# Attention on one core: two score tiles in three PSUM banks, and a third PSUM tile for the transposes

## The chip, the cores and the metric

The kernel runs on one core of a Trainium2 chip. The core has a matrix engine, TensorE (PE in the profile, with PEld for its weight loads), a vector engine (DVE), an activation engine (ACT), GpSimd (POOL) and a sync engine (SP) that here only issues DMAs. Each takes its instructions in the order in which they were laid down; they meet only at semaphores. TensorE writes its results to PSUM, eight banks of 512 float32 values for each of 128 partitions, and VectorE and ScalarE read them there. The metric is the device time of one execution in microseconds (us), the median of several runs.

## The reference

The reference is a two-layer backbone: in each layer a SwiGLU half step, a token mixer (a short convolution in layer 0, grouped-query attention in layer 1) and another SwiGLU half step, every one with a normalisation, a shift and scale before it and a gated residual behind it. 512 latent tokens attend to 768 keys, namely the 512 latent tokens and 256 context tokens. There are 8 query heads and 2 key-value heads of 128 values each. What bears on the change is the attention of one block of 128 queries:

```python
def gqa_block(q, k, v):
    s = jnp.einsum('bqkgd,bskd->bkgqs', q, k).astype(jnp.float32) * (HEAD_DIM ** -0.5)
    p = jax.nn.softmax(s, axis=-1).astype(v.dtype)
    return jnp.einsum('bkgqs,bskd->bqkgd', p, v)
...
    qb = q_l.reshape(b, n_blocks, Q_BLOCK, N_KV_HEADS, GQA_GROUP, HEAD_DIM).transpose(1, 0, 2, 3, 4, 5)
    o_l = lax.map(lambda q_blk: gqa_block(q_blk, k_all, v_all), qb)
    y_lat = o_l @ w_o
```

All of it is in float32; the order in which the keys are taken makes no difference to a softmax or to the weighted sum behind it.

## The kernel before, in words

To keep float32 accuracy every operand of a product is split into a high and a low part (`split`, L205: ScalarE copies the rounded high part, L206, VectorE subtracts it from the source, L207), and every product is three matmuls: high by high, low by high, high by low. Nearly all of the time is the feed-forward products; the attention of layer 1 lies at about 1894 to 2012 us of 2394.

The queries, keys and values are projected first (`qf`, `kh`, `kl`, `vh`, `vl`). Then comes the part that the change touches, `with tc.tile_pool(name="core" ...)` (L1521). It works on 32 blocks, 8 heads by 4 blocks of 128 queries. `blk` is the block in its head, and n counts the blocks from 0 to 31. Three functions make one block:

- `scores(h, blk)` (L1527): six matmuls write the scores of 128 queries by 768 keys to a tile `sc` with the tag C, three of 512 keys (`off` 0, the latent ones) and three of 256 (the context ones), at L1540 to L1542. Then VectorE takes the row maximum (`reduce_max`, L1544, 768 wide) and scales it (L1545), ScalarE takes the exponential with the row sum (L1547, reading the scores again), VectorE the reciprocal of the sum (L1548), and the probabilities `pr`, which lie in SBUF, are scaled by it, on VectorE for even blocks (L1552) and on ScalarE for odd ones (L1550). After the exponential the score tile is free.
- `turn(h, blk, pr)` (L1555): six transposes on TensorE (L1564) bring `pr` to keys by queries, three each into a PSUM tile with the tag T or U (here called a turn's half). Each tile is emptied by a `split` into `ph` and `pl` (L206, L207).
- `values(h, half, ph, pl)` (L1569): 18 matmuls (`mm3`, L883 to L885) multiply the transposed probabilities of two blocks by the values into a tile with the tag O, which is split into `oh` and `ol`.

TensorE's order is written out by hand in the loop at L1588: in iteration n come the scores of block n + 2, the turn of block n, and then, in every even iteration from 2 on, the values of blocks n - 2 and n - 1. From n = 17 on the odd iterations have a `filler` instead, a step of the output projection (12 matmuls of 512, tile `ps_A`). The first two blocks' scores come ahead of the loop, and behind them the last of the value projections (`v_chunk(5, ...)`, 24 matmuls, L1491 to L1493). TensorE and the DMA queue of SP are issued in program order (`ORDERED`, L47); on VectorE and ScalarE a scheduler lays the instructions down in the order in which it takes them to become ready.

The PSUM tiles come from pools, `psum(C=2, T=2, O=1)` and `psum(U=1)` (L1521, L1522). A tag's number is its number of tiles. A score tile is 1024 values wide, of which 768 are used, so it takes two banks: C has 4 banks, T has 2, O and U have 1 each, and together that is all eight. While h < 4 the halves of the turns go T, T, U in rotation (`turns[0] % 3`, L1562), so a tile is used again after three halves. After the fourth head U is closed and its bank goes to the filler. The tile framework sets the semaphore waits: whoever writes a tile waits for those who still read what was in it.

## Time and profile before

| what | value |
|---|---|
| median of 3 runs | 2396.28 us (2395.4 to 2396.76) |
| the profiled execution's own time | 2396.33 us |
| its span, from the first to the last instruction | 2394.0 us |
| TensorE busy over the span | 2372.9 us (99%) |
| VectorE, ScalarE busy over the span | 2031.4 us (85%), 1168.2 us (49%) |
| first matmul of the 1st, 3rd and 20th block's scores | 1894.04, 1899.40, 1950.61 us |
| TensorE's granted clock over the span | 0.999 |

The profile shows one execution. Its rows name a line of the kernel, an engine, an operation, and the tiles as out<-in with the buffer numbers left out; "ps_C" is a tile of the tag C. Matmuls are pipelined: a row's duration is longer than the step to the next row, and the step is what a matmul costs when they follow each other. In a timeline the square brackets give how long the engine was idle before the row, and whom it waited for. The exponential has two rows, the ACTIVATE and an ACTIVATION_READ_ACCUMULATOR that ends it by delivering the row sum.

### The profile page before, as it was taken

How to read it: one execution, taken by the hardware profiler on the slowest of the kernel's cores; microseconds unless marked ns; L12 is line 12 of the kernel's file. 1: busy time of each engine (PE TensorE's matmuls, PEld its weight loads, DVE VectorE, ACT ScalarE, POOL GpSimd, SP SyncE). 2: the span in 40 equal slices, each digit the busy share in tenths (PEclk: the TensorE clock that was granted, in tenths of full speed). 3: DMA queues.
4: the chain of work that ended last, by engine and by line, in shares of the span. 5: the costliest groups of instructions: out<-in, count | busy, mean ns of one | idle time of the engine just before them, and what ended most of it. 6: DMA issues, size and time to landing. Idle time of an engine off the chain costs nothing.

```text
span 2394.0 us, 37639 instructions
## 1 busy us (share of the span) xinstructions
PE 2372.9 (99%) x14303; PEld 2247.7 (94%) x14303; DVE 2031.4 (85%) x4018; ACT 1168.2 (49%) x2198; POOL 135.4 (6%) x256
## 2 busy tenths in 40 slices
PE   9999999999999999999999999999999999999998
PEld 6999999999999999999999999999998889899998
DVE  6989989978988888888887988888778987988887
ACT  5634334355535653433435543343355776555555
POOL 0001101100000001000000001101100000000000
PEclk9999999999999999999999999999999999999999
DMA  9234444430334123423432144444441101133331
GB/s 338 86 112 138 130 128 129 131 115 27 106 106 133 37 66 115 127 93 119 128 103 70 49 128 124 150 137 121 140 132 45 53 10 58 67 110 102 106 107 62
DMA packets 93062, 253.71 MB, mean 106 GB/s; under 512 B 10320, under 2 KB 18640, under 8 KB 92880
## 3 DMA queue, kind: packets, MB, share of 16 engines
q1 hardware_dynamic: 71984, 183.65, 23.8%
q0 software_dynamic: 20352, 67.12, 9.5%
q8 instruction: 112, 1.84, 0.3%
q14 instruction: 70, 0.57, 0.1%
q10 hardware_dynamic: 544, 0.52, 0.1%
HBM read 249.16 MB, written 2.10 MB: 105 GB/s over the span
## 4 chain that ended last, share of the span: by engine, by line
PE 90%; DVE 4%; ACT 3%; DMA 1%; issue 1%; SPq 0%; DVEq 0%; ACTq 0%
PE ps_A L883 16%; PE ps_A L884 16%; PE ps_A L885 16%; PE ps_C L883 11%; PE ps_C L884 11%; PE ps_C L885 11%; PE ps_B L885 3%; PE ps_B L883 3%; PE ps_B L884 3%; PE ps_T L1564 1%; DMA ada<-in_ada_w 0%; DVE f L785 0%; DVE w L207 0%; DMA raw<-in_ffn_w_in 0%; ACT pr L1547 0%
## 5 line engine op out<-in xcount | busy, mean ns | idle before, releaser
L206 ACT ACTIVATE w<-raw 128x512 fp32r<-128x512 f32 (+1 forms) x862 | 523.6, 621 | 708.9 <-PE ps_A L885 219.1
L207 DVE TENSOR_TENSOR w<-raw,w 128x512 fp32r<-128x512 f32 (+1 forms) x862 | 574.6, 680 | 118.0 <-ACT w L206 104.8
L526 POOL DMA_DIRECT2D aw<-in_ada_t x240 | 129.4, 539 | 1367.0 <-DVE mods L547 1078.5
L390 DVE TENSOR_TENSOR raw<-raw,raw 128x512 f32<-128x512 f32 x264 | 181.7, 690 | 9.0 <-DMA raw<-in_ffn_w_in 4.9
L884 PE MATMUL ps_C<-gl,w 128*128 128x512 f32 (+1 forms) x548 | 188.3, 344 | 0.0
L883 PE MATMUL ps_C<-gh,w 128*128 128x512 f32 (+1 forms) x548 | 188.1, 343 | 0.0
L885 PE MATMUL ps_C<-gh,w 128*128 128x512 f32 (+1 forms) x548 | 188.0, 343 | 0.0
L883 PE MATMUL ps_A<-gh,w 128*128 128x512 f32 (+1 forms) x540 | 185.5, 343 | 0.6 <-DVE x L951 0.6
L884 PE MATMUL ps_A<-gl,w 128*128 128x512 f32 (+1 forms) x540 | 185.6, 344 | 0.0
L885 PE MATMUL ps_A<-gh,w 128*128 128x512 f32 (+1 forms) x540 | 185.4, 343 | 0.0
L547 DVE CUSTOM_DVE_ANT_0 ps_S<-aw,silu_row,packed 128x512 f32<-128x512 f32 x208 | 157.1, 756 | 2.3 <-DMA aw<-in_ada_t 0.9
L547 DVE CUSTOM_DVE_ANT_0 ps_S<-aw,silu_row,mods 128x512 f32<-128x512 f32 x208 | 157.1, 755 | 1.0
L951 DVE SCALAR_TENSOR_TENSOR x<-ps_C,gat,x 128x512 f32<-128x512 f32 (+1 forms) x158 | 99.8, 633 | 43.8 <-PE ps_C L885 43.3
L883 PE MATMUL ps_A<-tB11h,w 128*128 128x384 f32 (+1 forms) x400 | 129.6, 324 | 0.2 <-ACT tB11h L807 0.2
L884 PE MATMUL ps_A<-tB11l,w 128*128 128x384 f32 (+1 forms) x400 | 129.1, 323 | 0.2 <-DVE tB11l L808 0.2
L885 PE MATMUL ps_A<-tB11h,w 128*128 128x384 f32 (+1 forms) x400 | 128.8, 322 | 0.0
L883 PE MATMUL ps_C<-tB22h,w 128*128 128x384 f32 (+2 forms) x376 | 121.3, 322 | 0.0
L885 PE MATMUL ps_C<-tB22h,w 128*128 128x384 f32 (+2 forms) x376 | 121.2, 322 | 0.0
L884 PE MATMUL ps_C<-tB22l,w 128*128 128x384 f32 (+2 forms) x376 | 121.2, 322 | 0.0
L951 DVE SCALAR_TENSOR_TENSOR x<-ps_A,gat,x 128x512 f32<-128x512 f32 (+1 forms) x162 | 102.1, 639 | 16.5 <-PE ps_A L885 16.3
L883 PEld LDWEIGHTS ps_A<-gh,w 128*128 128x128 f32 x540 | 102.3, 189 | 14.0 <-issue 1.0
L885 PEld LDWEIGHTS ps_C<-gh,w 128*128 128x128 f32 x548 | 103.8, 189 | 12.3
(486 smaller groups left out, 6931.9 us busy)
## 6 DMA issues: line engine op xcount, KB each, us to landing
raw<-in_ffn_w_in SPq DMA_DIRECT2D x170, 512.0 KB, 3.8
aw<-in_ada_t POOLq DMA_DIRECT2D x240, 256.0 KB, 3.0
raw<-in_ffn_w_out SPq DMA_DIRECT2D x80, 512.0 KB, 4.1
raw<-in_conv_w_in SPq DMA_DIRECT2D x24, 512.0 KB, 3.7
ada<-in_ada_w SPq DMA_DIRECT2D x28, 256.0 KB, 5.3
raw<-in_attn_w_qkv SPq DMA_DIRECT2D x12, 512.0 KB, 4.5
raw<-in_ada_w SPq DMA_DIRECT2D x8, 512.0 KB, 6.3
silu_row<-in_crow POOLq DMA_DIRECT2D x8, 512.0 KB, 4.1
```

The costliest lines, as they stand in the source:

```text
L206: hi = act.activation(dsth, src, AF.Copy)
L207: lo = dve.tensor_tensor(out=dstl, in0=src, in1=dsth.bitcast(F32), op=ALU.subtract)
L390: dve.tensor_tensor(out=quad(o), in0=quad(x), in1=quad(y), op=ALU.subtract)
L526: nc.gpsimd.dma_start(w, a["ada_t"][t, kh, j])
L547: ins = dve.tensor_tensor_reduce(out=junk, in0=w, in1=silu_row[kh][:, v, :], scale=1.0, scalar=total if kh else ada_b[:, i, hm // 2, col : ...
L883: pe.matmul(ps, wh, xh, start=first, stop=False, **kw)
L884: pe.matmul(ps, wh, xl, start=False, stop=False, **kw)
L885: pe.matmul(ps, wl, xh, start=False, stop=last, **kw)
L951: dve.scalar_tensor_tensor(out=x, in0=p[:, o - off : o - off + w], scalar=gat[:, m, v : v + 1], in1=x, op0=ALU.mult, op1=ALU.add)
L1564: pe.transpose(pt[:, c, :], pr[:, (c0 + c) * P : (c0 + c + 1) * P], ident)
```

## The change

The pools become `psum(C=1, T=3, O=1)`. There is now one tile with the tag C, 1536 values wide, which is exactly three banks, and it is made once for all 32 blocks (`both_sets`). Even blocks use its first 768 columns and odd blocks its last 768. So that no matmul's output crosses a bank, an odd block puts its 256 context keys first (columns 768 to 1023, the second half of the middle bank) and its 512 latent keys behind them (columns 1024 to 1535, the third bank); an even block puts 512 latent keys in the first bank and 256 context keys in the first half of the middle bank. `turn` picks each key block from where it now lies. The bank that becomes free is a third tile of the tag T, and the rotation while h < 4 is over four halves, T, T, T, U. The number of instructions that compute, and their sizes, stay as they were.

```diff
-        with tc.tile_pool(name="core", bufs=2) as cp, psum(C=2, T=2, O=1), ExitStack() as more:
+        with tc.tile_pool(name="core", bufs=2) as cp, psum(C=1, T=3, O=1), ExitStack() as more:
             more.enter_context(psum(U=1))
             turns = [0]
+            both_sets = ptile("C", (P, 2 * NT))
+            SETS = (((0, NL), (NL, NX)), ((NX, NL), (0, NX)))
...
-                sc = ptile("C", (P, 1024))[:, :NT]
-                for off, n in ((0, NL), (NL, NX)):
-                    p = sc[:, off : off + n]
+                side = blk % 2
+                sc = both_sets[:, side * NT : side * NT + NT]
+                for (at, n), off in zip(SETS[side], (0, NL)):
+                    p = sc[:, at : at + n]
...
-                    pt = ptile("U" if h < 4 and turns[0] % 3 == 0 else "T", (P, 4, P))[:, :3, :]
+                    pt = ptile("U" if h < 4 and turns[0] % 4 == 0 else "T", (P, 4, P))[:, :3, :]
                     for c in range(3):
-                        pe.transpose(pt[:, c, :], pr[:, (c0 + c) * P : (c0 + c + 1) * P], ident)
+                        key = (c0 + c) * P
+                        (lat_at, _), (ctx_at, _) = SETS[qq]
+                        key += lat_at if key < NL else ctx_at - NL
+                        pe.transpose(pt[:, c, :], pr[:, key : key + P], ident)
```

The built program shows what becomes of the waits. A name in brackets is the engine whose semaphore an instruction waits for, by the number of instructions that it has finished. In the changed kernel the lines of `scores` and `turn` have moved: L1540 to L1542 are now L1543 to L1545, the reduction L1544 is L1547, the scaling of the maximum L1545 is L1548, the exponential L1547 is L1550, the reciprocal L1548 is L1551, the scaling of even blocks L1552 is L1555, and the transposes L1564 are L1570.

First TensorE, at the end of the first block's scores and the begin of the second block's, before:

```order
L1540 MATMUL ps_C<-kh_17962,qh 128x256
L1541 MATMUL ps_C<-kl_17964,qh 128x256
L1542 MATMUL ps_C<-kh_17962,ql 128x256
L1540 MATMUL ps_C<-kh_17962,qh 128x512
L1541 MATMUL ps_C<-kl_17964,qh 128x512
```

and the same place with the change:

```order
L1543 MATMUL ps_C<-kh_17962,qh 128x256
L1544 MATMUL ps_C<-kl_17964,qh 128x256
L1545 MATMUL ps_C<-kh_17962,ql 128x256
L1543 MATMUL ps_C<-kh_17962,qh 128x512 [waits Activation_49]
L1544 MATMUL ps_C<-kl_17964,qh 128x512
```

The order of the matmuls is the same, but the first matmul of the second block's scores now waits for ScalarE, and the value that it waits for is that of the first block's exponential. It is so for all blocks: before, the scores of block m wait for the exponential of block m - 2, which read the same one of the two tiles; now they wait for that of block m - 1. The wait stands at the first of the six matmuls, ahead of the 512 keys and of the 256.

Then VectorE at the same place, from the first block's row maximum on, before:

```order
L1544 TENSOR_REDUCE sm<-ps_C 128x1 [waits DVE_49,PE_49]
L1544 TENSOR_REDUCE sm<-ps_C 128x1 [waits PE_49]
L1545 TENSOR_TENSOR sm<-sm,nrq 128x1 [waits DVE_49] x2
L1548 RECIPROCAL sm<-sm 128x1 [waits Activation_49]
L1552 TENSOR_SCALAR pr<-pr,sm 128x768 [waits DVE_49]
```

and with the change:

```order
L1547 TENSOR_REDUCE sm<-ps_C 128x1 [waits DVE_49,PE_49]
L1548 TENSOR_TENSOR sm<-sm,nrq 128x1 [waits DVE_49]
L1551 RECIPROCAL sm<-sm 128x1 [waits Activation_49]
L1555 TENSOR_SCALAR pr<-pr,sm 128x768 [waits DVE_49]
L1547 TENSOR_REDUCE sm<-ps_C 128x1 [waits PE_49]
```

The second block's row maximum has moved from ahead of the first block's reciprocal to behind the scaling of its probabilities.

Last TensorE's transposes of one odd block, in a middle iteration of the first four heads, before:

```order
L1564 MATMUL ps_T<-ident,pr 128x128 [waits PE_49,Activation_49]
L1564 MATMUL ps_T<-ident,pr 128x128 x2
L1564 MATMUL ps_T<-ident,pr 128x128 [waits DVE_49]
L1564 MATMUL ps_T<-ident,pr 128x128 x2
L1540 MATMUL ps_C<-kh_17962,qh 128x512 [waits Activation_49]
```

and with the change:

```order
L1570 MATMUL ps_T<-ident,pr 128x128 [waits PE_49]
L1570 MATMUL ps_T<-ident,pr 128x128 x2
L1570 MATMUL ps_U<-ident,pr 128x128 [waits PE_49]
L1570 MATMUL ps_U<-ident,pr 128x128 x2
L1543 MATMUL ps_C<-kh_17962,qh 128x512 [waits Activation_49]
```

The wait of a turn's half for VectorE, which had to empty the tile, is gone; what is left is a wait for TensorE's own earlier transposes into it.

## The prediction

> **What bounds the kernel now.** I read the page first: the busy shares, the slices of the clock, and the chain that ended last.

> ```profile
> PE 2372.9 (99%) x14303; PEld 2247.7 (94%) x14303; DVE 2031.4 (85%) x4018; ACT 1168.2 (49%) x2198; POOL 135.4 (6%) x256
> ...
> PEclk9999999999999999999999999999999999999999
> ...
> PE 90%; DVE 4%; ACT 3%; DMA 1%; issue 1%; SPq 0%; DVEq 0%; ACTq 0%
> ```

> TensorE carries the whole span at full clock. A change elsewhere can win only where TensorE stands still, and it loses wherever it makes TensorE stand still. So next come the windows, cut where the attention changes character: its start, the first four heads, and the heads with the filler. The columns are the stretch, its length, then busy time (instructions) of PE, PEld, DVE, ACT and POOL, the granted clock, and the DMA's share and rate.

> ```profile
> 1893.00:1910.00 17.00, 16.27 (x115) 14.52 (x114) 14.41 (x38) 12.56 (x29) 0.00 (x0) 1.00 0.19 61
> 1910.00:1930.00 20.00, 19.27 (x139) 17.16 (x137) 17.30 (x42) 16.53 (x35) 0.00 (x0) 1.00 0.01 1
> 1930.00:1950.00 20.00, 19.25 (x141) 17.43 (x140) 17.81 (x44) 16.48 (x36) 0.00 (x0) 1.00 0.01 2
> 1950.00:1970.00 20.00, 20.00 (x132) 18.21 (x131) 15.89 (x36) 14.63 (x30) 0.00 (x0) 1.00 0.00 1
> ```

> TensorE is idle for 17.00 - 16.27 + 20.00 - 19.27 + 20.00 - 19.25 = 2.21 us up to 1950, and not at all behind it. Ends of matmuls are modelled, so I also take the chain of waits, over 1880 to 2030 (total us, times, longest):

> ```profile
> PEld ps_T L1564 <- DVE p L207: 2.7, 7, 0.6
> ...
> PE ps_T L1564 <- DVE p L207: 0.9, 3, 0.4
> ...
> PEld ps_U L1564 <- DVE p L207: 0.8, 2, 0.5
> PEld ps_C L1540 <- ACT pr L1547: 0.8, 2, 0.5
> ...
> PE ps_U L1564 <- DVE p L207: 0.3, 1, 0.3
> PE ps_C L1540 <- ACT pr L1547: 0.2, 1, 0.2
> ```

> The transposes wait for VectorE to empty their PSUM tile: 2.7 + 0.9 + 0.8 + 0.3 = 4.7 us over weight loads and matmuls. So the third tile can win between 2.2 and 4.7 us. The scores hardly wait for the exponential, 0.8 + 0.2 us, all of it at the start; two score tiles take turns.

> **The change, part by part.** *What it removes* is that wait of the transposes, at most 4.7 us. *What it adds* is in the built program: the scores of a block now wait for the exponential of the block just before. The question is how long it is from a block's first score matmul to the end of its exponential, and what TensorE has to do meanwhile. The clearest place is the block that starts at 1955.09, where no engine has a backlog. First TensorE, from its scores over the turn to the next block's scores:

> ```profile
> 1955.09 0.39 PE L1540 MATMUL ps_C<-kh,qh 128*128 128x512 f32 x1
> ...
> 1956.13 0.82 PE L1564 MATMUL ps_T<-ident,pr 128*128 128x128 f32 x6
> 1956.70 0.36 PE L883 MATMUL ps_O<-p,vh 128*128 128x256 f32 x1
> ...
> 1958.93 0.40 PE L1540 MATMUL ps_C<-kh,qh 128*128 128x512 f32 x1
> ```

> then VectorE and ScalarE on the same block:

> ```profile
> 1956.33 0.96 DVE L1544 TENSOR_REDUCE sm<-ps_C 128x1 f32<-128x768 f32 x1 [0.28 <-PE ps_C L1542]
> 1957.20 0.55 DVE L207 TENSOR_TENSOR p<-ps_T,p 128x384 fp32r<-128x384 f32 x1
> 1957.66 0.15 DVE L1545 TENSOR_TENSOR sm<-sm,nrq 128x1 f32<-128x1 f32 x1
> ```

> ```profile
> 1957.85 0.99 ACT L1547 ACTIVATE pr<-ps_C,sm,rq 128x768 f32<-128x768 f32 x1 [0.32 <-DVE sm L1545]
> 1958.75 0.19 ACT L1547 ACTIVATION_READ_ACCUMULATOR pr<-ps_C,sm,rq 128x1 f32 x1
> ```

> Scores take 1956.13 - 1955.09 = 1.04 us of TensorE, the turn 0.57, the values 1958.93 - 1956.70 = 2.23. The exponential ends at 1958.75 + 0.19 = 1958.94, 3.85 us after its scores began: the scores until VectorE can start (1.24), the reduction to the next step (0.87), one split that stands between (0.46), the scaling with its hand-over to ScalarE (0.19), and the exponential with its row sum (1.09). In the changed program the same split stands between the reduction and the scaling. What a wait for the exponential adds behind its end shows at one of the first blocks:

> ```profile
> 1903.17 0.22 ACT L1547 ACTIVATION_READ_ACCUMULATOR pr<-ps_C,sm,rq 128x1 f32 x1
> ```

> ```profile
> 1903.44 0.50 PE L1540 MATMUL ps_C<-kh,qh 128*128 128x512 f32 x1 [0.21 <-ACT pr L1547]
> ```

> 0.05 us after 1903.39, and the first matmul has a row of 0.50 instead of 0.39 or 0.40, about 0.1 us. So from one block's scores to the next there are 3.85 + 0.05 = 3.90 us at least, and up to 4.00 where the start is slow; I take 3.95. It holds for iterations with values too: TensorE's own 1.04 + 0.57 + 2.23 = 3.84 us just fails to fill it.

> *The first heads.* Without values or filler TensorE has 1.04 + 0.57 = 1.61 us of work, and that is what an odd iteration takes now, as these three starts of scores show (an odd one is 1.63, an even one 4.57 with its stalls):

> ```profile
> 1913.91 0.40 PE L1540 MATMUL ps_C<-kh,qh 128*128 128x512 f32 x1
> ...
> 1915.54 0.48 PE L1540 MATMUL ps_C<-kh,qh 128*128 128x512 f32 x1
> ...
> 1920.11 0.40 PE L1540 MATMUL ps_C<-kh,qh 128*128 128x512 f32 x1
> ```

> Afterwards the odd one takes 3.95, with 2.3 us of idle TensorE, since the turn is all that stands ahead of the next scores, and everything else queues behind the waiting matmul: the turn and the values that VectorE and ScalarE would work on next. The even one falls from about 4.4 to 3.95, for its stalls are the removed ones and the engines have no backlog any more. The stretch from the third block's scores to the twentieth's is 17 iterations without filler:

> ```profile
> 1899.40 0.50 PE L1540 MATMUL ps_C<-kh,qh 128*128 128x512 f32 x1
> ...
> 1950.61 0.40 PE L1540 MATMUL ps_C<-kh,qh 128*128 128x512 f32 x1
> ```

> That is 51.21 us now, and 17 x 3.95 = 67.15 then: +15.9 us. The gain of the third tile is in it and gets no second credit.

> *The start.* The second block's scores come right behind the first's now and would wait for its exponential:

> ```profile
> 1895.20 0.40 PE L1540 MATMUL ps_C<-kh,qh 128*128 128x512 f32 x1
> ...
> 1896.25 0.28 PE L1491 MATMUL ps_O<-w,h 128*128 128x256 f32 x1
> ```

> ```profile
> 1896.22 1.82 DVE L1544 TENSOR_REDUCE sm<-ps_C 128x1 f32<-128x768 f32 x2
> 1897.95 0.28 DVE L1545 TENSOR_TENSOR sm<-sm,nrq 128x1 f32<-128x1 f32 x2
> ```

> ```profile
> 1898.27 0.99 ACT L1547 ACTIVATE pr<-ps_C,sm,rq 128x768 f32<-128x768 f32 x1 [2.80 <-issue]
> ```

> Two reductions and two scalings stand ahead of the first exponential now, one of each afterwards, so it starts 0.87 + 0.07 us earlier, at 1897.33, ends 1.09 later, and the second scores start at 1898.47, 3.27 us late. The 24 matmuls of the value projection that follow (1896.25 on, 0.12 us a step, 2.88 us) start at 1899.6 and end at 1902.5; the third block's scores start there instead of at 1899.40. Its own exponential is over by then (1898.47 + 3.85 = 1902.3). +3.1 us.

> *The heads with the filler.* An odd iteration has 12 matmuls more, so TensorE is busy past 3.95 and the wait costs nothing: 1955.09 ends the interval of such a one, which began with the scores at 1950.61, 4.48 us. The even ones go from 3.84 (1955.09 to 1958.93) to 3.95; there are six with scores behind them: 6 x 0.1 = +0.6 us. No stall is left there that a third tile could take away.

> *Moved elsewhere*: nothing. The order of TensorE, SP and POOL is otherwise the same, and what follows the attention is TensorE's again:

> ```profile
> 2050.00:2100.00 50.00, 48.14 (x351) 44.88 (x351) 48.71 (x92) 29.78 (x65) 0.00 (x0) 1.00 0.23 77
> 2100.00:2200.00 100.00, 100.00 (x688) 93.11 (x687) 81.98 (x148) 52.70 (x106) 0.00 (x0) 1.00 0.33 110
> ```

> so the delay goes through to the end, but for the 50.00 - 48.14 = 1.9 us of idle TensorE there, which could take up some of it.

> **The sum.** 15.9 + 3.1 + 0.6 = 19.6 us on the profiled execution's 2396.33, which is 0.05 above the median: 2415.9 us. The unknown is the interval. At the least the split falls behind the scaling, 3.85 - 0.46 + 0.05 = 3.44 for odd iterations, and the even ones stay at TensorE's 3.84: mean 3.65, 17 x 3.65 = 62.05, so +10.8 + 3.1, and if the 1.9 us are taken up too, +12: 2408. At the most it is as long as with today's backlog, where the block of 1913.91 has its exponential end at 1918.23:

> ```profile
> 1918.04 0.19 ACT L1547 ACTIVATION_READ_ACCUMULATOR pr<-ps_C,sm,rq 128x1 f32 x1
> ```

> 4.32 + 0.05 = 4.37 for all: 74.3 - 51.2 = +23.1, with 3.1 and 6 x 0.5 in the filler's even ones +29: 2425. Between these I stay with the unbacklogged row, because VectorE and ScalarE have the same work in a longer stretch.

> [...] The order shows the wait ahead of all six, so the sum goes by that.

> **Rivals.** *Faster:* the wait is met before TensorE comes to it, and only the gain of the third tile is left. Place: every odd iteration of the first four heads; price: -2.2 to -4.7 us, about 2393. It decides if a block's exponential ends within the 1.6 us that scores and turn take. Against it is the chain, 3.85 us even with idle engines, of which reduction and exponential alone are 0.87 + 1.09. Chance 0.03. *No change:* the order is right but the idle time lies in today's stalls and behind the attention (2.2 + 1.9 us), and the engines' shorter queues give back the rest; that would need 15 us more than these rows have. Chance 0.03. *Much slower:* the clock. The rows show it at 1.00 throughout, but nowhere in the attention idle gaps of 2.3 us in each pair of iterations, or 3.3 us at the start. If it fell to half for these 17 iterations, the scores would add 1.04 us to each odd one (4.99) and an even one would take 2 x 3.84 = 7.68: mean 6.34, 17 x 6.34 = 107.8, +56.6 + 3.1: about 2456. Chance 0.06. [...]

> **How the numbers follow.** The forecast, one score tile in effect, has 0.88, faster and no change 0.03 each, the clock 0.06. The range of the forecast, 2408 to 2425, leaves out the 0.12 of the rivals and a little of its own. A measurement here can tell about 0.2% (4.8 us) from no change, and both ends of the forecast's range are beyond that: slower 0.88 + 0.06 = 0.94, same 0.03, faster 0.03.

> **What would show it.** In the profile after: waits of "ps_C" matmuls for the exponential, some 20 us over the attention and the longest about 3 us at the start; score starts 3.9 to 4.0 us apart in the first heads; the waits of transposes for VectorE gone; TensorE busy about 70% between 1902 and 1970, and all as before behind it. Wrong it would be if the scores' starts still alternate 1.6 and 4.4, if the interval is set by another engine's queue, or if the clock's slices fall below 9.

## The result, and the profile after

| | median | lowest to highest | runs |
|---|---|---|---|
| before | 2395.98 us | 2395.40 to 2396.76 | 4 |
| after | 2427.62 us | 2426.23 to 2428.79 | 4 |

The changed kernel takes 1.0132 times as long (95% interval 1.0121 to 1.0144): it is 31.6 us slower, where 19.6 us were forecast, and the time lies 2.6 us above the range. The profiled execution of after took 2428.79 us, 32.5 us more than that of before (2396.33).

The page of after, with the busy shares, the slices of TensorE and of its clock, and the chain:

```profile
PE 2384.9 (98%) x14303; PEld 2259.1 (93%) x14303; DVE 2035.6 (84%) x4018; ACT 1170.6 (48%) x2198; POOL 135.0 (6%) x256
...
PE   8999999999999999999999999999999789999998
...
PEclk9999999999999999999999999999999989999999
...
PE 91%; DVE 4%; ACT 3%; DMA 1%; issue 1%; SPq 0%; DVEq 0%; ACTq 0%
```

Two slices of TensorE in the attention fall to 7 and 8, and one slice of the clock to 8; before, the clock was 9 throughout. The last line of the prediction names just that among the signs of being wrong. The windows over the attention of after show both together (stretch, length, busy time and instructions of PE, PEld, DVE, ACT and POOL, granted clock, DMA share and rate):

```profile
1893.00:1910.00 17.00, 11.92 (x74) 10.64 (x73) 10.04 (x26) 8.09 (x18) 0.00 (x0) 0.90 0.22 63
1910.00:1930.00 20.00, 15.35 (x90) 13.98 (x87) 12.54 (x27) 12.13 (x24) 0.00 (x0) 0.83 0.00 1
1930.00:1950.00 20.00, 13.96 (x86) 12.65 (x87) 13.09 (x30) 12.82 (x25) 0.00 (x0) 0.91 0.00 0
1950.00:1975.00 25.00, 20.20 (x125) 18.63 (x123) 15.82 (x34) 14.90 (x29) 0.00 (x0) 0.86 0.00 1
1990.00:2044.00 54.00, 54.00 (x345) 48.42 (x344) 41.12 (x88) 35.28 (x71) 0.00 (x0) 1.00 0.09 30
```

TensorE has idle time now in every stretch without the filler, and the mean clock there is 0.83 to 0.91. With the filler (last row) it is busy throughout and at full clock. The waits over 1880 to 2060 (total us, times, longest) tell who is waited for:

```profile
PEld ps_C L1543 <- ACT pr L1550: 24.5, 10, 3.5
...
PE ps_C L1543 <- ACT pr L1550: 22.1, 10, 3.3
```

The scores wait for the exponential, 22.1 us in ten places, the longest 3.3; no row of transposes that wait for VectorE is left. Those are the waits that the prediction named. Here is one block in the timeline of after, from its scores to the next block's, and on to the one after that:

```profile
1918.26 0.40 PE L1543 MATMUL ps_C<-kh,qh 128*128 128x512 f32 x1
...
1919.52 0.96 DVE L1547 TENSOR_REDUCE sm<-ps_C 128x1 f32<-128x768 f32 x1 [0.22 <-PE ps_C L1545]
...
1920.40 0.55 DVE L207 TENSOR_TENSOR p<-ps_T,p 128x384 fp32r<-128x384 f32 x1
1920.86 0.15 DVE L1548 TENSOR_TENSOR sm<-sm,nrq 128x1 f32<-128x1 f32 x1
...
1921.11 0.99 ACT L1550 ACTIVATE pr<-ps_C,sm,rq 128x768 f32<-128x768 f32 x1 [0.39 <-DVE sm L1548]
1922.00 0.19 ACT L1550 ACTIVATION_READ_ACCUMULATOR pr<-ps_C,sm,rq 128x1 f32 x1
...
1922.24 0.50 PE L1543 MATMUL ps_C<-kh,qh 128*128 128x512 f32 x1 [2.10 <-ACT pr L1550]
...
1924.98 0.41 PE L884 MATMUL ps_O<-p,vh 128*128 128x256 f32 x1
...
1925.19 0.41 PE L885 MATMUL ps_O<-p,vl 128*128 128x256 f32 x1
...
1927.05 0.28 PE L883 MATMUL ps_O<-p,vh 128*128 128x256 f32 x1
...
1927.16 0.28 PE L884 MATMUL ps_O<-p,vh 128*128 128x256 f32 x1
...
1927.76 0.39 PE L1543 MATMUL ps_C<-kh,qh 128*128 128x512 f32 x1
```

The first interval is the predicted one, piece by piece: 1.26 us to the reduction (1.24 foreseen), 0.88 for it, a split of 0.46 between, 0.25 to the exponential, 1.08 for it (1921.11 to 1922.19), and 0.05 to the next scores: 3.98 us. The second interval is 5.52 us, and no matmul in it waits so long. The values' matmuls in its middle follow each other by 0.21 us (1924.98 to 1925.19), those at its end by 0.11 (1927.05 to 1927.16). Windows cut where the clock changes say why:

```profile
1919.85:1923.27 3.42, 1.32 (x8) 0.94 (x7) 1.79 (x5) 2.80 (x5) 0.00 (x0) 1.00 0.01 2
1923.27:1926.68 3.41, 3.41 (x18) 3.41 (x17) 2.16 (x5) 2.15 (x5) 0.00 (x0) 0.50 0.02 5
1926.68:1930.09 3.41, 2.94 (x22) 2.56 (x21) 2.28 (x5) 1.60 (x4) 0.00 (x0) 1.00 0.00 0
```

Behind a stretch of 3.4 us in which TensorE was busy for 1.32, the clock is 0.50 for one such stretch and then full again. In after this happens seven times, at 1899.37, 1913.03, 1923.27, 1940.33, 1950.57, 1967.64 and 1977.88, always whole multiples of 3.41 us apart. An even iteration has 3.84 us of work and about 0.2 us to spare. At half clock 3.41 / 2 = 1.7 us of that work is put off, and so about 1.5 us are lost, which is what the row shows (5.52 instead of 4.0).

### The profile page after: what moved, and what is told of

Its sections match the earlier page's. It is cut to its first block, busy times and chain, and to the rows that moved or that the text cites. A ratio compares the mean times of both kernels' runs of the same rounds, so it can differ in the third digit from the quotient of the medians.

```text
span 2426.6 us, 37640 instructions
## 1 busy us (share of the span) xinstructions
PE 2384.9 (98%) x14303; PEld 2259.1 (93%) x14303; DVE 2035.6 (84%) x4018; ACT 1170.6 (48%) x2198; POOL 135.0 (6%) x256
## 4 chain that ended last, share of the span: by engine, by line
PE 91%; DVE 4%; ACT 3%; DMA 1%; issue 1%; SPq 0%; DVEq 0%; ACTq 0%
PE ps_A L883 16%; PE ps_A L884 16%; PE ps_A L885 16%; PE ps_C L883 11%; PE ps_C L884 10%; PE ps_C L885 10%; PE ps_B L885 3%; PE ps_B L883 3%; PE ps_B L884 2%; PE ps_T L1570 1%; PE ps_C L1543 1%; PE ps_O L883 1%; PE ps_O L884 1%; PE ps_O L885 1%; PE ps_C L1545 1%
## 5 line engine op out<-in xcount | busy, mean ns | idle before, releaser
L207 DVE TENSOR_TENSOR w<-raw,w 128x512 fp32r<-128x512 f32 (+1 forms) x862 | 573.8, 678 | 117.5 <-ACT w L206 104.3
L883 PE MATMUL ps_C<-gh,w 128*128 128x512 f32 (+1 forms) x548 | 188.1, 343 | 0.0
L883 PE MATMUL ps_A<-gh,w 128*128 128x512 f32 (+1 forms) x540 | 185.5, 343 | 0.6 <-DVE x L951 0.6
L883 PE MATMUL ps_A<-tB11h,w 128*128 128x384 f32 (+1 forms) x400 | 129.6, 324 | 0.2 <-ACT tB11h L807 0.2
L883 PE MATMUL ps_C<-tB22h,w 128*128 128x384 f32 (+2 forms) x376 | 121.3, 323 | 0.0
L883 PEld LDWEIGHTS ps_A<-gh,w 128*128 128x128 f32 x540 | 102.3, 189 | 14.0 <-issue 1.0
```

Of the source, the lines that this page charges most:

```text
L207: lo = dve.tensor_tensor(out=dstl, in0=src, in1=dsth.bitcast(F32), op=ALU.subtract)
L883: pe.matmul(ps, wh, xh, start=first, stop=False, **kw)
```

## The experiments

The theories are these. *The wait:* one score tile means that the scores of a block wait for the exponential of the block just before, and all of the loss comes from there, part directly and part through the clock. *The shared bank:* the two halves of a bank, or the other key order, cost something by themselves. *The third tile:* it gives some of the loss back, or costs something. *The clock:* the single stretches at half clock are an effect of TensorE's idle time, and give back about 9 us if that is filled. In the expectations, theory 1 is the wait together with the clock, rival 1 is the third tile, rival 2 the shared bank, and rivals 3 and 3a are other readings of the clock; theories 4 and 5 are about the transposes' stalls in the kernel before. All kernels of one batch stood beside runs of the kernel before, with medians of 2395.3 to 2395.5 us.

**The change without the third tile** (against after):

```diff
-        ... psum(C=1, T=3, O=1), ExitStack() as more:
+        ... psum(C=1, T=2, O=1), ExitStack() as more:
-                    pt = ptile("U" if h < 4 and turns[0] % 4 == 0 else "T", (P, 4, P))[:, :3, :]
+                    pt = ptile("U" if h < 4 and turns[0] % 3 == 0 else "T", (P, 4, P))[:, :3, :]
```

> The change with the third transpose tile undone: T=2 and the rotation over three halves as before, the shared three-bank score tile kept. Theory 1 (the scores wait for the exponential of the block just before, and the idle time that this opens lets the clock fall to half in single windows of 3.41 us): nothing of the delay comes from the transposes, so as with the whole change, 2427 us, within 2. Rival 1 (the new rotation of the transposes' tiles costs or wins): back by several us, towards 2396 if it is the cause.

Measured: 2427.19 us (2426.48 to 2428.76), ratio 1.0134 (1.0117 to 1.0151), beside 2427.62 with the third tile. It does nothing here, either way.

**The kernel before with one score tile** (one character; two banks, no bank shared, the old key order):

```diff
-        ... psum(C=2, T=2, O=1), ExitStack() as more:
+        ... psum(C=1, T=2, O=1), ExitStack() as more:
```

> The kernel before with one score tile instead of two (C=1, two banks) and nothing else: no shared bank, keys in their old order, transposes as before. Theory 1: the wait alone is the change, so 2427 us, within 3, score starts 4.0 us apart at full clock in the first heads and 5.5 where a half-clock window falls. Rival 2 (TensorE writing to one half of the middle bank while VectorE and ScalarE read the other costs time): clearly less than the change, 2410 or below.

Measured: 2427.74 us (2427.1 to 2428.57), ratio 1.0135 (1.0119 to 1.015). The loss is all there without any of the change's addressing. The shared bank and the key order cost nothing that can be seen (2427.62 us with them, in after). One thing differs from after: at the start the clock stays at half for two stretches, not one.

```profile
1893.60:1897.02 3.42, 1.40 (x9) 1.04 (x7) 3.05 (x9) 1.44 (x4) 0.00 (x0) 1.00 0.23 84
1897.02:1900.43 3.41, 2.13 (x7) 1.85 (x8) 0.79 (x2) 1.08 (x2) 0.00 (x0) 0.50 0.54 151
1900.43:1903.84 3.41, 3.41 (x18) 3.41 (x18) 1.28 (x3) 1.73 (x3) 0.00 (x0) 0.50 0.01 2
...
1910.67:1914.08 3.41, 1.53 (x10) 1.42 (x11) 2.07 (x7) 2.39 (x4) 0.00 (x0) 1.00 0.00 0
1914.08:1917.50 3.42, 3.42 (x27) 3.19 (x26) 2.70 (x7) 2.34 (x5) 0.00 (x0) 1.00 0.00 0
```

The first half-clock stretch has TensorE busy for 2.13 us, and the next one is still at half; later, 1.53 us at full clock are enough for the next one to stay at full. In the loop this kernel has five half-clock stretches, where after has six.

**One tile of four banks**, its two sides 1024 columns apart, so that they are in separate banks (against before):

```diff
-        ... psum(C=2, T=2, O=1), ExitStack() as more:
+        ... psum(C=1, T=2, O=1), ExitStack() as more:
+            both_sets = ptile("C", (P, 2048))
...
-                sc = ptile("C", (P, 1024))[:, :NT]
+                sc = both_sets[:, blk % 2 * 1024 : blk % 2 * 1024 + NT]
```

> One score tile of four banks, the two sides 1024 columns apart, so no bank is shared; keys in their old order, T=2. In the built program the scores still wait for the exponential of the block just before, though they write to other banks than it reads. Theory 1: 2427 us, within 3. Rival 2 (the shared bank is what costs, or what the wait is for): near 2396.

Measured: 2427.62 us (2427.48 to 2428.05), ratio 1.0134 (1.0119 to 1.0149). Its waits on TensorE have the same row as after's, at its own line numbers:

```profile
PE ps_C L1541 <- ACT pr L1548: 22.1, 10, 3.3
```

The score tile has the four banks that the two tiles of before had together, and the columns of two blocks that follow each other have no bank in common, yet the scores wait. So the wait goes here by the tile that was allocated, not by the columns or the bank that a block uses. What a change that only shared the bank would cost can't be read from this, since the tile's wait covers it and no run here has two engines at one bank at once.

**Filling TensorE's idle time** (against the kernel without the third tile; F is a PSUM tile that nothing reads, so these matmuls are additional work, without use). 16 matmuls of 128x256 go behind the first block's scores and behind the turn of each odd block up to the 15th:

```diff
-        ... psum(C=1, T=2, O=1), ExitStack() as more:
+        ... psum(C=1, T=2, O=1, F=1), ExitStack() as more:
...
+            fill_tile = ptile("F", (P, 256))
...
-            ready = [scores(*blocks[0]), scores(*blocks[1])]
+            def busy(count):
+                for k in range(count):
+                    pe.matmul(fill_tile, kh[0][:, :P], kh[0][:, :256], start=True, stop=True)
+
+            ready = [scores(*blocks[0])]
+            busy(16)
+            ready.append(scores(*blocks[1]))
...
                 elif n > 16:
                     next(filler, None)
+                elif n % 2:
+                    busy(16)
```

> As a_shared_T2, and in the idle time 16 matmuls of 128x256 (about 1.9 us) whose result nobody reads: behind the first block's scores, and behind the transposes of each odd block up to the 15th. The wait stays, the idle time is filled. Theory 1: no half-clock window between 1890 and 1990, all score starts 4.0 to 4.1 us apart in the first heads, 10 to 11 us less than a_shared_T2: 2417, within 2. Rival 3 (the clock rows are only a sign of idle time, the delay is the waits' alone): as a_shared_T2, 2427, or more.

Measured: 2418.78 us (2418.47 to 2419.23), ratio 1.0097 (1.0082 to 1.0112). With more work the kernel is 8.4 us faster than without. Its windows, the same stretches as above:

```profile
1910.00:1930.00 20.00, 19.31 (x143) 17.85 (x142) 13.42 (x31) 13.61 (x27) 0.00 (x0) 1.00 0.00 1
1930.00:1950.00 20.00, 19.57 (x146) 18.19 (x145) 13.84 (x32) 13.00 (x27) 0.00 (x0) 1.00 0.01 2
```

The clock is 1.00. What is left is the wait alone, and it can be read from the score starts of this kernel (first block, third, twentieth, last):

```profile
1893.99 0.50 PE L1544 MATMUL ps_C<-kh,qh 128*128 128x512 f32 x1
...
1902.64 0.40 PE L1544 MATMUL ps_C<-kh,qh 128*128 128x512 f32 x1
...
1971.29 0.50 PE L1544 MATMUL ps_C<-kh,qh 128*128 128x512 f32 x1
...
2022.11 0.50 PE L1544 MATMUL ps_C<-kh,qh 128*128 128x512 f32 x1
```

**Less filling, 8 and 4 matmuls** in the same places:

```diff
-            busy(16)
+            busy(8)
...
-                    busy(16)
+                    busy(8)
```

> As d_fill16 with 8 matmuls of 128x256 in each place instead of 16, about 0.95 us. [...] Theory 1, with that share as the threshold: the windows of the first heads, 0.19 at the least, rise to 0.44 and stay at full clock; the window at the start, empty but for them, has 0.25 and is followed by half clock: one or two half-clock windows, at 1895 to 1905, 2419 to 2421 us. Rival 3a (only a window without idle time in it keeps the clock): six or more half windows, 2427.

> As d_fill16 with 4 matmuls in each place, 0.125 of a window. Theory 1: the lowest windows get to 0.32 and most of the others over 0.37, so between none and four half-clock windows in the first heads, and one or two at the start; 2420 to 2426 us, and each half window in the loop costs 1.5 us.

Measured: 2418.77 us (2418.0 to 2420.25) with 8, and 2419.63 (2418.89 to 2420.25) with 4, which is 0.4 us below what I had expected. With 8 I had expected a half-clock stretch or two at the start, and there is none in its profile: a miss. TensorE does stand still there for 2.35 us (1.48 in the first of the two stretches below, 0.87 in the second), longer than the 2.10 us that went ahead of a half-clock stretch in after. But counted back in steps of 3.413 us from the fall of the clock at the end of its trace (2409.36; in after there are 153 such steps from 1899.37 to the fall at its end, 2421.61), a border of two stretches lies inside this gap, so neither is nearly empty:

```profile
1893.95:1897.36 3.41, 1.93 (x14) 1.64 (x12) 2.77 (x7) 1.35 (x4) 0.00 (x0) 1.00 0.27 70
1897.36:1900.77 3.41, 2.54 (x18) 2.41 (x19) 1.90 (x4) 0.82 (x2) 0.00 (x0) 1.00 0.37 130
```

With 4 there is a half-clock stretch at the start:

```profile
1895.90:1899.31 3.41, 1.13 (x6) 0.99 (x7) 1.74 (x4) 1.08 (x2) 0.00 (x0) 1.00 0.55 154
1899.31:1902.73 3.42, 3.42 (x18) 3.42 (x17) 1.28 (x3) 1.67 (x3) 0.00 (x0) 0.50 0.03 7
```

From the fourth block's scores to the twentieth's the intervals of that kernel are 4.0 to 4.1 us. Four small matmuls per pair of blocks, half a microsecond of work in 8 (4 steps of 0.12 us), were enough to keep the clock at 1.00 in the loop, where the stretch with the least work has 1.73 us of busy TensorE. So here a gap as such didn't lower it, since gaps are still there, and neither did the length of a gap alone (2.35 us with 8): what the stretches differ in is how much work is left in them. With one gap in a stretch at full clock, the work in it and the part of the gap that falls into it are the same measure, and these runs don't tell them apart. The shares of a stretch in these two expectations, with 0.37 as the limit, were my estimate, and no run shows them; what the traces show is busy time, in after 1.32 us (0.39 of a stretch) ahead of half clock and 1.64 us (0.48) ahead of full clock.

**What a further transpose tile could be worth at all.** The third tile could not show its gain behind the new wait. With two score tiles there is no bank for it, so the other direction was tried, one tile fewer than before (U unused, T alone, two tiles):

```diff
-                    pt = ptile("U" if h < 4 and turns[0] % 3 == 0 else "T", (P, 4, P))[:, :3, :]
+                    pt = ptile("T", (P, 4, P))[:, :3, :]
```

> The kernel before with the transposes on the two tiles of the tag T alone, also in the first four heads (the tile U stays unused): one tile less in rotation instead of one more. Theory 5 (what holds the first heads back is the row maximum, the exponential and the scaling of the probabilities on VectorE and ScalarE; the number of tiles only decides at which instruction TensorE meets it): within 2 us of before. Theory 4 (the stalls of the transposes are from too few tiles): the wait of each half comes a half earlier, 0.3 to 0.6 us in each of 16 iterations, 2400 to 2405.

Measured: 2397.2 us (2396.45 to 2397.84, 11 runs), ratio 1.0007 (0.9998 to 1.0016). That is within the 2 us of theory 5, and below the 2400 to 2405 of theory 4: three tiles are worth 1.7 us over two, if that. Its waits on TensorE:

```profile
PE ps_T L1564 <- DVE p L207: 2.5, 8, 0.3
PE ps_T L1564 <- DVE sm L1545: 0.4, 1, 0.4
```

The matmuls' wait for VectorE rises from the 1.2 us of before (0.9 + 0.3) to 2.5. From this a fourth tile can hardly win more than the step from two to three did. That is argued from one side; four tiles beside two score tiles weren't tried.

**Three ways around the transposes' stalls in the kernel before**, to see whether those stalls are time that can be had. First, in even iterations up to 14, the second half of the turn goes behind the values, so that it meets its tile later:

```diff
-                p = turn(h, blk, ready[n])
+                p = turn(h, blk, ready[n], (0,) if late and n < 16 else (0, 3))
...
                     values(*late)
+                    if n < 16:
+                        turn(h, blk, ready[n], (3,))
```

> The kernel before, with two score tiles, and in the even iterations up to n = 14 the second half of the turn laid behind the values instead of ahead of them: the half that waits for VectorE to empty its tile gets 2.2 us more time, with no PSUM at all. Theory 4 (the stalls of the transposes, 2.2 to 4.7 us in the profile of before, are what could be won here): 2391 to 2393.5, faster by 0.1 to 0.2%. Rival 4a (VectorE's own work sets the pace of the first heads, and the stall only moves to the next wait): within 1 us of before.

Second, in even iterations up to 16, the whole turn behind the values:

```diff
+                late_first = late and n <= 16
+                if late_first:
+                    values(*late)
                 p = turn(h, blk, ready[n])
...
-                    values(*late)
+                    if not late_first:
+                        values(*late)
```

> The kernel before, with the whole turn behind the values in the even iterations up to n = 16. Theory 4: as f_split_turn, 2391 to 2393.5. Rival 4b: the values now come 0.6 us sooner and wait for the splits of the block before, as much as the transposes waited: within 1 us of before, or slower.

Third, the scaling of the probabilities of even blocks on GpSimd, to relieve VectorE:

```diff
-                    dve.tensor_scalar_mul(pr, pr, sm[:, 3:4])
+                    nc.gpsimd.tensor_scalar_mul(pr, pr, sm[:, 3:4])
```

> The kernel before with the scaling of the even blocks' probabilities (0.62 us on VectorE) moved to GpSimd, which is idle there. Theory 5: VectorE has 0.62 us less in each pair of blocks, and the stalls of the first heads shrink by the 2 to 4 us that they have: 2392 to 2394.5. Rival 5a: GpSimd takes longer for the same than VectorE, and its end comes later at the transposes that wait for it: as before or slower.

Measured: 2397.78 us (11 runs), ratio 1.0010 (1.0001 to 1.0019); 2402.53 (6 runs), 1.0030 (1.0019 to 1.0042); 2397.01 (11 runs), 1.0005 (0.9997 to 1.0014). None gains, the first loses 2.4 us and the second 7.2. The gains that theories 4 and 5 expected came in none of the three, and the first is slower than its rival allowed, too. Their waits on TensorE, in this order:

```profile
PE ps_T L1564 <- DVE sm L1545: 2.3, 5, 0.5
PE ps_U L1564 <- DVE sm L1545: 1.0, 2, 0.5
PE ps_T L1564 <- DVE p L207: 0.9, 1, 0.9
```

```profile
PE ps_O L884 <- DVE p L207: 4.8, 6, 0.8
PE ps_T L1564 <- DVE p L207: 3.5, 2, 2.2
```

```profile
PE ps_T L1564 <- POOL pr L1552: 3.7, 6, 1.7
PE ps_T L1564 <- DVE p L207: 0.3, 1, 0.3
```

In the first and the third the wait for VectorE's splits (L207) gets smaller and another takes its place: the matmuls wait until after the scaling of the row maximum (L1545), or for GpSimd. In the second the waits for the splits grow, at the transposes and at the values. So the idea that the stalls can be had by one of these orders falls. It fits that TensorE meets a chain through VectorE and ScalarE at one tile or the other, as theory 5 has it, but that isn't shown: none of these kernels takes work out of the chain, since on GpSimd the scaling takes 2.2 us instead of 0.62.

## Why the prediction was right about the cause and wrong about the size

These are the first matmuls of the scores in after, for the first block, the third, the twentieth and the last; the third to the twentieth are the 17 iterations of the main term, the twentieth to the last those with the filler:

```profile
1894.79 0.50 PE L1543 MATMUL ps_C<-kh,qh 128*128 128x512 f32 x1
...
1904.94 0.40 PE L1543 MATMUL ps_C<-kh,qh 128*128 128x512 f32 x1
...
1982.10 0.40 PE L1543 MATMUL ps_C<-kh,qh 128*128 128x512 f32 x1
...
2032.81 0.50 PE L1543 MATMUL ps_C<-kh,qh 128*128 128x512 f32 x1
```

In the kernel before the last block's scores stand here:

```profile
2000.33 0.40 PE L1540 MATMUL ps_C<-kh,qh 128*128 128x512 f32 x1
```

The terms against the kernel before, with the filled kernel (16 matmuls) as the one that shows the wait without the clock:

| term | predicted | wait alone (filled kernel) | after |
|---|---|---|---|
| up to the third block's scores | +3.1 | 1902.64 - 1899.40 = +3.24 | 1904.94 - 1899.40 = +5.54 |
| 17 iterations (51.21 us before) | +15.9 | 68.65 - 51.21 = +17.44 | 77.16 - 51.21 = +25.95 |
| 12 iterations with the filler (49.72 us before) | +0.6 | 50.82 - 49.72 = +1.10 | 50.71 - 49.72 = +0.99 |
| sum | +19.6 | +21.8 | +32.5 |

*The direction and the cause held.* One score tile in effect, the wait at the first of the six matmuls, the idle time in odd iterations and at the start, the transposes' waits gone without a gain of their own, nothing given back behind the attention (from the last block's scores to the end it takes 2394.0 - 2000.33 = 393.7 us before and 2426.6 - 2032.81 = 393.8 after): each is in the profile, and the kernel before with one tile alone gives the whole loss. The rivals "faster" and "no change" fell with it.

*The step that failed is the judgement on the clock.* The prediction priced half clock as all or nothing over the 17 iterations (2456 us) and gave it 0.06; the sum of the forecast has no term for the clock. In the runs the answer came stretch by stretch, for 3.41 us at a time, and it went with the work in the stretch ahead. In after, and in the kernel without the third tile, every such stretch with at most 1.32 us of busy TensorE was followed by one at half clock, and none with 1.64 us or more; the kernel before with one score tile narrows that to 1.40 and 1.53 us. The trace of before has half clock only at its end, 0.50 from 2388.50 on, behind 3.41 us without a matmul. A stretch that falls around 2.3 us of idle time has only 3.41 - 2.3 = 1.1 us of work in it; but the length of the stretches was first seen in after, and no row of before shows that a stretch with so much work is followed by half clock. What it costs is six times 1.5 us in the loop less a little (77.16 - 68.65 = 8.5 us) and 1.5 of the 2.3 us by which the two starts differ; the rest of the 2.3 is scatter ahead of the attention (the first scores begin 0.8 us later in after than in the filled kernel). By medians, filling the gaps gives 2427.19 - 2418.78 = 8.4 us.

The half-clock stretches lie on one grid: the seven of after begin multiples of 3.41 us apart. The stretches ahead of them weren't all idle: in the loop 1.25 to 1.32 us of busy time stood in them, and the first matmuls of a block's scores (1922.24) among it.

*The interval was slightly undersized:* 68.65 / 17 = 4.04 us instead of 3.95, which is 1.5 us over 17 iterations. The upper bound that the prediction worked out for an unbacklogged chain, 4.00, lay nearer: most intervals begin behind a wait, with the slow first matmul (a row of 0.50 instead of 0.40, and 0.34 us instead of 0.23 to the next row), and the hand-over to ScalarE was 0.25 rather than 0.19. For the same reason the heads with the filler cost 1.0 instead of 0.6: the even iterations there take 3.89 us instead of 3.84, and the odd ones behind them about 4.58 instead of 4.44, most of it the slow first matmul with which they now begin. With these alone the time would have been 2396.3 + 21.8 = 2418, inside the range.

*The ceiling of the third tile* was read too high. The 4.7 us add the waits of the weight loads to those of the matmuls behind them, which stand still at the same time (up to 1917.57 for 0.50 and 0.26 us); the matmuls' waits for the splits are 0.9 + 0.3 = 1.2 us, and all of TensorE's idle time there is 2.21. The sum gave the tile no credit of its own, so the forecast doesn't hang on it.

*The wait ahead of all six matmuls* was rightly read from the order: the kernel with its two sides in separate banks has the same 22.1 us of waits and the same time (2427.62 us) as the other kernels with one tile (2427.19 to 2427.74).

## What to carry to other kernels

Slices of one PSUM tile didn't double-buffer here (22.1 us of waits, also with four banks): before two buffers are packed into one, look in the built program whether the writer's wait still skips a turn, since it may go by the tile that was allocated and not by the columns. When a change makes TensorE wait inside a loop, add up its work in every stretch of 3.4 us rather than looking for the longest gap; here a stretch at full clock with at most 1.40 us of busy time was followed by one at half clock, and the wait cost more than its length (31.6 us, against 2418.78 - 2395.35 = 23 with the gaps filled). A stall that the profile shows at a buffer may only be where a chain is met, so price another buffer by removing one first; that is cheap, but it answers from one side only.

## What the runs showed of the hardware that was not expected

```profile
L1552 POOL TENSOR_SCALAR pr<-pr,sm 128x768 f32<-128x768 f32 x16 | 35.3, 2205 | 141.5 <-DVE sm L1548 141.5
```

```profile
L1552 DVE TENSOR_SCALAR pr<-pr,sm 128x768 f32<-128x768 f32 x16 | 9.9, 619 | 0.4
```
